# One-directional filter tiles with sums and differences of halves, and another order at front, gates and maxima

## The chip, the core and the metric

The kernel runs on one core of a Trainium2 chip. The metric is the device time of one execution in microseconds; the time before is a median of three runs. Five engines work side by side, each through its own instructions in order: TensorE (PE, with its weight loads on PEld), VectorE (DVE), ScalarE (ACT), GpSimd (POOL) and SyncE (SP, which issues nearly all of the transfers here). In this kernel PE's products go to PSUM, from where the other engines read them, and many matrix products are sums of products of high and low parts in the type fp32r.

## What is computed

Two layers over 1024 latent tokens of width 1024 with 256 context tokens. Layer 0 is attention (grouped-query heads and latent-attention heads side by side, a SiLU gate, one output projection), layer 1 is a Hyena mixer with long convolutions. The part that the change touches most makes the filters of these convolutions, which depend on no token:

```python
hid = sin(freq * (emb @ w1 + b1)); hid = sin(freq * (hid @ w2 + b2))
h = (hid @ w3 + b3).reshape(L, HY_ORDER, 2, HY_WIDTH)
h = h * exp(-t * abs(deltas))[:, None, None, :]
fwd, bwd = h[:, :, 0], h[:, :, 1]
kern = concatenate([fwd, zeros((1, HY_ORDER, HY_WIDTH)), bwd[:0:-1]], axis=0)   # 2048 taps
kern = kern / sum(abs(kern), axis=0, keepdims=True)
return rfft(kern, axis=0)
```

In attention, the scores of a group are exponentiated after a row maximum is taken off; the gate is `silu(h @ w_gate)`.

## The kernel before

**Filters (up to about 255 us).** A small MLP gives `hid` for the 1024 positions (`sin_arg` on DVE, Sin on ACT). `hidden(q)` puts it into tiles of 128 partitions, the forward positions in one half and the backward ones in the other, as high part `Hh` and low part `Hl`. The loop at L604 then runs over 38 steps: 8 blocks of 128 channels by 4 quarters of the taps, and 6 steps to drain. Step n does, on the engines in this order:

- `taps(n)` (L472): PE, four outputs of 128x256, each from four products: the bias `ind`·`b4` (L479) and the three of `mm3` (L100 to L102).
- `decay(n + 1)` (L530): ACT, four exponentials into `dec`, of which there are two buffers.
- `second_stage` and `spectra`: PE multiplies regrouped data by `FBk` (L572); DVE scales by the reciprocal norm into `kc` (L583), which is written to DRAM. This works on an earlier block.
- `decayed(n)` (L535): DVE, `kern` = taps times decay, 128x1024.
- `first_stage(n - 1)`: PE multiplies two halves of `kern` by `FKc` (L557), ACT copies to `aT` (L559).
- `norms(n)`: ACT takes absolute values of two halves (L544), POOL adds them up (L546, L550).
- a regrouping by DMA through SP, the reciprocal `rn` once per block (L647), and `split_coefs` once per block: high and low parts of `w3` and the bias (ACT L339 and L342, POOL L340, DVE L343). `coefs` loads them.

With each step go pieces of other work, pulled from generators. `mods` multiplies the adaLN weights (32 tiles of 512 KB through SP, `adaw`) on PE (L217); `PM` says how many of its pieces go where in the MLP, and one is pulled in each step. `stats` takes the tokens' norms in steps 0 to 11. `toks` prepares tokens from step 11 on: DVE scales a tile (L402), PE transposes half of it (L408), ACT modulates it in four pieces into `mraw` (L413), DVE casts it to the high part (L420), POOL makes the low part (L421). Steps 12 to 31 are called the token steps below.

**Gates (about 378 to 480 us).** Sixteen tiles, each of 24 products. `load(n)` fetches a weight tile, ACT casts it to `wh` (L803), POOL (n under 8) or DVE subtracts the low part `wl` (L804), all right before tile n - 1 is multiplied. The rotary work of POOL and DVE (L838, L839, L840) runs in the same stretch.

**Attention (about 480 to 1010 us).** 32 groups gi of five slices s. In the last slice (s = 4), `max_rows(gi + 1)` has PE transpose the next group's maxima `m` (L1023) between the two halves `scores(0)` and `scores(1)`; DVE has reduced them to `m` (L1008) just ahead. Once, near 745 us, the weights `uvr` of the values are scaled and cast on ACT and their low part `uvl` subtracted on POOL (L1508), before PE multiplies with it (L101).

The order of each engine is fixed when the program is built: a scheduler of streams takes the pieces by their costs and due times (`yield cost, delay`).

Of the kernel before, what the change touches and what calls it, by code (L numbers as in the profile page):

```python
# [2294 lines left out]
```

## Time and profile before

| | us |
|---|---|
| median of three runs (lowest, highest) | 1813.27 (1812.65, 1813.64) |
| profiled execution | 1815.76 |
| its span, first to last instruction | 1813.9 |
| PE busy in it | 1727.4 (95%) |
| DVE, ACT, POOL busy | 1075.8 (59%), 775.1 (43%), 819.9 (45%) |
| mean granted clock of PE | 0.984 |

The profiled execution lies 2.5 us above the median. The profile is read by stage: a view of stretches says which engine is full, a view of lines what one instruction takes, the view in order of time who waits for whom; the number in brackets is the idle time ahead of an instruction and its releaser. PE's matmuls overlap, so a duration of 0.28 us can stand at a distance of 0.12.

### The profile page before, as it was taken

The numbers are of one execution on the slowest core, as the hardware profiler recorded it, in microseconds if no ns is written. First come the engines' busy times: TensorE is split into PE (matmuls) and PEld (weight loads), VectorE is DVE, ScalarE is ACT, GpSimd is POOL, SyncE is SP. The second block draws the span as 40 slices with busy tenths as digits, with TensorE's granted clock in tenths as the row PEclk, the third lists the DMA queues.
The fourth block names the chain that finished last, engine by engine and source line by source line (L and its number), as shares of the span: only waits on it lengthen the run. The fifth ranks groups of instructions, "written<-read, shape, count | busy, mean of one in ns | idle before, by whom it ended". The sixth has DMA issues, their size and how long they took to land. (4 is left out here: it accounts for less than half of the span.)

```text
span 1813.9 us, 25833 instructions
## 1 busy us (share of the span) xinstructions
PE 1727.4 (95%) x9616; PEld 1349.0 (74%) x9616; DVE 1075.8 (59%) x1575; ACT 775.1 (43%) x1326; POOL 819.9 (45%) x583
## 2 busy tenths in 40 slices
PE   7889999998999999899999999999999999999898
PEld 2677788986766666566666788888888887888786
DVE  4557747636765666366656323555776667766843
ACT  3877721243545545544444333333333433333431
POOL 1457732434179777677777453233322223233200
PEclk8999999999999999999999999999999999999999
DMA  7766678322220010101001226556676675785533
GB/s 251 227 201 224 214 239 269 117 70 70 54 59 24 13 38 18 50 23 35 19 22 33 79 82 150 141 147 205 185 215 184 192 199 166 199 246 180 168 101 108
DMA packets 236493, 236.50 MB, mean 130 GB/s; under 512 B 29567, under 2 KB 194343, under 8 KB 235951
## 3 DMA queue, kind: packets, MB, share of 16 engines
q1 hardware_dynamic: 234192, 232.75, 42.4%
q10 hardware_dynamic: 2176, 2.10, 0.4%
q8 instruction: 76, 1.25, 0.3%
q14 instruction: 49, 0.40, 0.1%
HBM read 152.87 MB, written 61.94 MB: 118 GB/s over the span
## 5 line engine op out<-in xcount | busy, mean ns | idle before, releaser
L990 DVE TENSOR_REDUCE mx<-pq 128x1 f32<-128x512 f32 x256 | 170.8, 682 | 113.1 <-PE pq L989 111.2
L1294 ACT ACTIVATE PT<-pw 128x1024 f32<-128x1024 f32 x160 | 163.7, 1025 | 171.8 <-PE pw L1277 157.4
L100 PE MATMUL pw<-h1h,wh 128*128 128x512 f32 x512 | 208.9, 408 | 0.0
L102 PE MATMUL pw<-h1h,wl 128*128 128x512 f32 x512 | 201.6, 394 | 0.0
L101 PE MATMUL pw<-h1l,wh 128*128 128x512 f32 x512 | 200.3, 391 | 0.0
L1189 POOL TENSOR_TENSOR acc<-acc,PT 128x1024 f32<-128x1024 f32 x62 | 147.4, 2377 | 22.3 <-ACT PT L1294 20.7
L1712 POOL TENSOR_TENSOR wl<-wr,wh 128x1024 fp32r<-128x1024 f32 x32 | 76.9, 2405 | 139.8 <-ACT wh L1711 129.5
L102 PEld LDWEIGHTS pw<-h1h,wl 128*128 128x128 f32 x512 | 96.4, 188 | 21.4
L546 POOL TENSOR_TENSOR kacc<-kacc,kabs 128x512 f32<-128x512 f32 x56 | 72.4, 1293 | 86.9 <-ACT kabs L544 85.0
L101 PEld LDWEIGHTS pw<-h1l,wh 128*128 128x128 f32 x512 | 96.8, 189 | 17.8
L100 PEld LDWEIGHTS pw<-h1h,wh 128*128 128x128 f32 x512 | 96.8, 189 | 17.4
L1187 POOL TENSOR_TENSOR acc<-PT,PT 128x1024 f32<-128x1024 f32 x31 | 73.9, 2385 | 53.8 <-ACT PT L1294 50.5
L1847 POOL TENSOR_TENSOR K<-K,skp 128x512 f32<-128x512 f32 x32 | 42.5, 1330 | 122.4 <-DMA K<-Kd 119.9
L1860 DVE TENSOR_TENSOR cA<-pq,K 64x512 f32<-64x512 f32 x128 | 88.1, 688 | 1.8
L1856 DVE SCALAR_TENSOR_TENSOR cB<-pq,K 64x512 f32<-64x512 f32 x64 | 44.3, 693 | 73.5 <-PE pq L1853 37.1
L1827 ACT COPY caT<-pq 128x512 f32<-128x512 f32 x64 | 37.6, 588 | 117.3 <-PE pq L102 107.0
L572 PE MATMUL pq<-au,FBk 128*128 128x256 f32 x256 | 68.1, 390 | 12.1 <-DVE kc L583 10.6
L1875 ACT COPY cbT<-pq 128x512 f32<-128x512 f32 x64 | 37.5, 587 | 97.3 <-PE pq L1873 68.1
L1873 PEld LDWEIGHTS pq<-cA,GB 128*128 128x128 f32 x512 | 67.3, 193 | 15.0 <-issue 10.0
L1180 PE MATMUL pv<-PT,Va 128*64 128x256 f32 x640 | 77.9, 385 | 0.0
L1180 PE MATMUL pv<-PT,Vm 128*64 128x256 f32 x640 | 77.7, 385 | 0.0
L1873 PE MATMUL pq<-cA,GB 128*128 128x128 f32 x512 | 68.8, 278 | 7.6 <-DVE cA L1863 6.6
(450 smaller groups left out, 4730.6 us busy)
## 6 DMA issues: line engine op xcount, KB each, us to landing
au<-aT SPq DMA_DIRECT2D x128, 128.0 KB
space<-in_ada_w_dram SPq DMA_DIRECT2D x32, 512.0 KB
wr<-in_hy_w_in_dram SPq DMA_DIRECT2D x32, 512.0 KB
K<-Kd SPq DMA_DIRECT2D x64, 256.0 KB
ad<-caT SPq DMA_DIRECT2D x64, 256.0 KB
cau<-ad SPq DMA_DIRECT2D x32, 512.0 KB
bd<-cbT SPq DMA_DIRECT2D x32, 512.0 KB
spare<-bd SPq DMA_DIRECT2D x64, 256.0 KB
```

The costliest lines, as they stand in the source:

```text
L100: nc.tensor.matmul(ps, lh, rh, start=start, stop=False)
L101: nc.tensor.matmul(ps, lh, rl, start=False, stop=False)
L102: nc.tensor.matmul(ps, ll, rh, start=False, stop=stop)
L546: nc.gpsimd.tensor_tensor(accs[p], accs[p], ab, ALU.add)
L990: nc.vector.reduce_max(m[:, i, j:j + 1], ps, axis=AX.X)
L1180: nc.tensor.matmul(ps[64 * e:64 * e + 64, 0:256], vals[:, 2 * s + j], PT[:, j, 256 * e:256 * e + 256], start=s == 0 and j == 0, stop=s == ...
L1187: eng.tensor_tensor(accs[gi], prev, PT, ALU.add)
L1189: eng.tensor_tensor(accs[gi], accs[gi], PT, ALU.add)
L1294: nc.scalar.activation(PT, ps.rearrange("p (a q) -> p a q", q=512), AF.Exp, scale=SC_A if kind == 0 else SC_M)
L1712: nc.gpsimd.tensor_tensor(wl, f(r), f(wh), ALU.subtract)
L1860: nc.vector.tensor_tensor(A1[64 * e:64 * e + 64], pv[64 * e:64 * e + 64], K[:, 0], ALU.mult)
L1873: nc.tensor.matmul(ps[:, i * P:(i + 1) * P], GB[:, 4 * uc + i, :], A1[:, i, :], start=True, stop=True)
```

## The change

**Filters.** Each tile of taps now holds positions of one direction only (d is forward or backward), with all 128 partitions used for high and low part together: `HA` holds the high part in one half and the low part in the other, `HB` the high part and rows of ones. So an output takes two products (`HA`·`WA`, `HB`·`WB`) where it took four, 8 for 16 in a step. `halves` has POOL make the sum and the difference of the two directions, and `first_stage` multiplies these. The norm is one DVE reduction of absolute values per step, over four taps at a stride of 256 elements, and one POOL add. `dec` has one buffer, and its four exponentials are issued as two pairs, each ahead of an `aT` copy. `split_coefs` has six ACT casts for two, two POOL and two DVE subtractions, and comes a step later; `coefs` comes one block ahead.

**Front.** `PM` is smaller, `mods` is pulled twice in steps 0 to 2, and the parts of `hidden` are issued between the two `sin_arg`.

**Gates, maxima, values.** A raw gate tile is loaded one tile earlier, and POOL subtracts only for tiles 2, 4 and 6. In groups of odd gi, `max_rows` follows `scores(1)`. `uvl` is subtracted on DVE. Constants change with the layout.

```diff
-PM = 3, 3, 5, 3
+PM = 2, 1, 3, 3
...
     def split_coefs(p):
         w3r, b3r, dl = coef[p]
-        w3h = fp.tile([P, CB], F32R, tag="w3h", bufs=2, name=nm("w3h"))
-        w3l = fp.tile([P, CB], F32R, tag="w3l", bufs=2, name=nm("w3l"))
-        nc.scalar.copy(w3h, w3r)
-        nc.gpsimd.tensor_tensor(w3l, w3r, f(w3h), ALU.subtract)
-        b4 = b4s[p % 2]
-        nc.scalar.copy(b4[0:2], b3r)
-        nc.vector.tensor_tensor(b4[32:34], b3r, f(b4[0:2]), ALU.subtract)
-        coef[p] = w3h, w3l, b4, dl
+        wa = fp.tile([P, 2, CB], F32R, tag="WA", bufs=2, name=nm("WA"))
+        wb = WB[p % 2]
+        for i in range(2):
+            a = slice(64 * i, 64 * i + 64)
+            for h in (a, slice(64 - 64 * i, 128 - 64 * i)):
+                nc.scalar.copy(wa[h, i], w3r[a])
+            nc.gpsimd.tensor_tensor(wb[a, i], w3r[a], f(wa[a, i]), ALU.subtract)
+            b_ = 64 * (1 - i)
+            nc.scalar.copy(wb[b_:b_ + 1, i], b3r[b_:b_ + 1])
+            nc.vector.tensor_tensor(wb[b_ + 32:b_ + 33, i], b3r[b_:b_ + 1], f(wb[b_:b_ + 1, i]), ALU.subtract)
+        coef[p] = wa, wb, dl
...
         def taps(n):
             p, gq = steps[n]
-            w3h, w3l, b4, _ = coef[p]
+            wa, wb, _ = coef[p]
             pws[n] = pw()
             for i in range(4):
-                g = 4 * gq + i
+                d, g = i // 2, 2 * gq + i % 2
                 pv = pws[n][:, i * CB:(i + 1) * CB]
-                nc.tensor.matmul(pv, ind, b4, start=True, stop=False)
-                mm3(nc, pv, Hh[:, g], Hl[:, g], w3h, w3l, False, True)
+                nc.tensor.matmul(pv, HA[:, d, g], wa[:, d], start=True, stop=False)
+                nc.tensor.matmul(pv, HB[:, d, g], wb[:, d], start=False, stop=True)
...
         def hidden(q):
-            c = slice(8 * q, 8 * q + 8)
-            for h in hs:
-                nc.scalar.activation(Hr[h, c, h], args[q][h, :].rearrange("p (g m) -> p g m", m=64), AF.Sin)
-            nc.scalar.copy(Hh[:, c], Hr[:, c])
-            (nc.vector, nc.gpsimd)[q].tensor_tensor(Hl[:, c], Hr[:, c], f(Hh[:, c]), ALU.subtract)
-
+            c = slice(4 * q, 4 * q + 4)
+            a = args[q].rearrange("p (g m) -> p g m", m=P)
+            nc.scalar.activation(a, a, AF.Sin)
+            for d, h in enumerate(hs):
+                nc.scalar.copy(HA[h, d, c], a[h])
+                nc.gpsimd.tensor_copy(HB[h, d, c], HA[h, d, c])
+                nc.vector.tensor_tensor(HA[hs[1 - d], d, c], a[h], f(HA[h, d, c]), ALU.subtract)
+
+        split_coefs(0)
         args[1] = sin_arg(pss[1], b2)
-        nc.scalar.copy(ind, indr)
-        split_coefs(0)
+        hidden(1)
         args[0] = sin_arg(pss[0], b2)
-        hidden(1)
         hidden(0)
...
-        def decay(n):
+        def decay(n, d):
+
             if n < len(steps):
                 p, gq = steps[n]
-                decs[n] = fw.tile([P, 4, P], F32, tag="dec", bufs=2, name=nm("dec"))
-                for j in range(4):
-                    nc.scalar.activation(decs[n][:, j], coef[p][-1], AF.Exp, scale=tng[:, 4 * gq + j:4 * gq + j + 1])
+                if d == 0:
+                    decs[n] = fw.tile([P, 4, P], F32, tag="dec", bufs=1, name=nm("dec"))
+                for j in range(2 * d, 2 * d + 2):
+                    t = j // 2 * NT + 2 * gq + j % 2
+                    nc.scalar.activation(decs[n][:, j], coef[p][-1], AF.Exp, scale=tng[:, t:t + 1])
...
         def norms(n):
+
             p, gq = steps[n]
+            t = fw.tile([P, CB], F32, tag="kacc" if gq == 3 else "kabs", bufs=2 if gq == 3 else 1, name=nm("kabs"))
+            nc.vector.tensor_reduce(t, kns[n].rearrange("p (g c) -> p c g", g=4), AX.X, ALU.add, apply_absolute_value=True)
             if gq == 3:
-                accs[p] = fw.tile([P, 512], F32, tag="kacc", bufs=1, name=nm("kacc"))
-            for i in range(2):
-                ab = accs[p] if gq == 3 and i == 0 else fw.tile([P, 512], F32, tag="kabs", bufs=2, name=nm("kabs"))
-                nc.scalar.activation(ab, kns[n][:, 512 * i:512 * i + 512], AF.Abs)
-                if ab is not accs[p]:
-                    nc.gpsimd.tensor_tensor(accs[p], accs[p], ab, ALU.add)
+                accs[p] = t
+            else:
+                nc.gpsimd.tensor_tensor(accs[p], accs[p], t, ALU.add)
             if gq == 0:
-                acc = accs.pop(p)
-                sums[p] = fw.tile([P, CB], F32, tag="ksum", bufs=1, name=nm("ksum"))
-                nc.gpsimd.tensor_tensor(sums[p], acc[:, :CB], acc[:, CB:], ALU.add)
+                sums[p] = accs.pop(p)
+
+        def halves(n):
+
+            a, b = kns[n][:, :512], kns[n][:, 512:]
+            sds[n] = [fw.tile([P, 512], F32, tag=t, bufs=1, name=nm(t)) for t in ("sum", "dif")]
+            for t, op_ in zip(sds[n], (ALU.add, ALU.subtract)):
+                nc.gpsimd.tensor_tensor(t, a, b, op_)
...
             ps = pq()
-            nc.tensor.matmul(ps, FKc, kns[n][:, j * 512:(j + 1) * 512], start=True, stop=True)
-            g = 4 * gq + 2 * j
-            nc.scalar.copy(aTs[p][:, g:g + 2, :], ps.rearrange("p (g c) -> p g c", c=CB))
+            nc.tensor.matmul(ps, FKc[:, j], sds[n][j], start=True, stop=True)
+            nc.scalar.copy(aTs[p][:, j, 2 * gq:2 * gq + 2, :], ps.rearrange("p (g c) -> p g c", c=CB))
...
-            decay(n + 1)
             if n >= 6:
                 ps0 = second_stage(pb, ub, 0)
             if n < N:
                 decayed(n)
+            decay(n + 1, 0)
             if n >= 6:
                 spectra(pb, ub, 0, ps0)
             if 0 < n <= N:
                 first_stage(n - 1, 0)
+            decay(n + 1, 1)
+            if 0 < n <= N:
                 first_stage(n - 1, 1)
             if n < N:
+                halves(n)
                 norms(n)
...
-                if q == 1 and p + 1 < NT:
+                if q == 0 and p + 1 < NT:
+                    coefs(p + 1)
+                if q == 2 and p + 1 < NT:
                     split_coefs(p + 1)
-                if q == 2 and p + 2 < NT:
-                    coefs(p + 2)
             if n == 2:
                 nc.sync.dma_start(FBk, I["FBk"])
-            pull(mods)
+            pull(mods, 2 if n < 3 else 1)
...
-                    (nc.gpsimd if n < 8 else nc.vector).tensor_tensor(wl, r, f(wh), ALU.subtract)
+                    (nc.gpsimd if n in (2, 4, 6) else nc.vector).tensor_tensor(wl, r, f(wh), ALU.subtract)
...
-                load(n + 1)
+                split(n + 1)
+                load(n + 2)
...
-                if s == 4 and gi + 1 < 32:
+                if s == 4 and gi % 2 == 0:
                     max_rows(gi + 1)
-                    cost += 0.1
                 scores(1, todo)
+                if s == 4 and gi % 2 and gi + 1 < 32:
+                    max_rows(gi + 1)
...
-        nc.gpsimd.tensor_tensor(uvl, r, f(uvh), ALU.subtract)
+        nc.vector.tensor_tensor(uvl, r, f(uvh), ALU.subtract)
```

On PE at the front, before: the rest of the adaLN products ahead of the first taps (L217 `pada` from the loads `adaw`; L497 is the MLP; `pw` the taps' bank).

```order
L217 MATMUL pada_181<-adaw_178,sT 32x512 x2
L217 MATMUL pada_181<-adaw_182,sT 32x512 x2
L217 MATMUL pada_181<-adaw_186,sT 32x512 x2
L497 MATMUL pq_214<-h_40_212,w_131 64x512 x2
L217 MATMUL pada_181<-adaw_190,sT 32x512 x2
L217 MATMUL pada_181<-adaw_199,sT 32x512 x2
L217 MATMUL pada_181<-adaw_203,sT 32x512 x2
L217 MATMUL pada_181<-adaw_208,sT 32x512 x2
L217 MATMUL pada_181<-adaw_217,sT 32x512 x2
L479 MATMUL pw_269<-b_111,ind 128x256
L100 MATMUL pw_269<-w3h_247,Hh 128x256
```

And now:

```order
L499 MATMUL pq_189<-h_34_187,w_132 64x512 x2
L217 MATMUL pada_178<-adaw_173,sT 32x512 x2
L499 MATMUL pq_198<-h_37_196,w_132 64x512 x2
L217 MATMUL pada_178<-adaw_175,sT 32x512 x2
L217 MATMUL pada_178<-adaw_179,sT 32x512 x2
L217 MATMUL pada_178<-adaw_183,sT 32x512 x2
L483 MATMUL pw_256<-WA_215,HA 128x256
L484 MATMUL pw_256<-WB_110,HB 128x256
L483 MATMUL pw_256<-WA_215,HA 128x256
```

The first taps stand behind 6 loads of `adaw`, where they stood behind 11; five of them follow later.

On ACT in one token step, before (`mraw` the modulated token, `kabs` the absolute values):

```order
L530 ACTIVATE dec_1370<-dlt_874,tng 128x128 x4
L559 COPY aT_1305<-pq_1383 128x512 [waits PE_49]
L559 COPY aT_1305<-pq_1386 128x512 [waits PE_49]
L544 ACTIVATE kabs_1389<-kern_1378 128x512 [waits DVE_49,Pool_49]
L544 ACTIVATE kabs_1392<-kern_1378 128x512 [waits Pool_49]
L413 ACTIVATE mraw_1417<-pq_1412,shl_504,scl_505 128x128 [waits PE_49]
L413 ACTIVATE mraw_1417<-pq_1412,shl_504,scl_505 128x128 x3
```

And now, in a step that also splits the coefficients (`WA`, `WB`):

```order
L536 ACTIVATE dec_1254<-dlt_911,tng 128x128 [waits DVE_49,Activation_49]
L536 ACTIVATE dec_1254<-dlt_911,tng 128x128
L569 COPY aT_1195<-pq_1260 128x512 [waits PE_49]
L536 ACTIVATE dec_1254<-dlt_911,tng 128x128 x2
L569 COPY aT_1195<-pq_1265 128x512 [waits PE_49]
L345 CAST WA_1286<-w3r_1154 64x256 x2
L348 CAST WB_111<-b3r_1156 1x256 [waits DMAHW0_49]
L345 CAST WA_1286<-w3r_1154 64x256 x2
L348 CAST WB_111<-b3r_1156 1x256
L419 ACTIVATE mraw_1302<-pq_1297,shl_581,scl_582 128x128 [waits PE_49,Pool_49]
L419 ACTIVATE mraw_1302<-pq_1297,shl_581,scl_582 128x128 x3
```

The absolute values are gone, the decays stand in two pairs with a wait for DVE ahead of the first, and six casts lie between the second `aT` and the token.

On POOL where the low part `uvl` was made, before (L1189 adds up the exponentials of attention, L1250 scales an output):

```order
L1187 TENSOR_TENSOR acc_7009<-PT_6950,PT_6972 128x1024 [waits DVE_49,Activation_49]
L1189 TENSOR_TENSOR acc_7009<-acc_7009,PT_7004 128x1024 [waits Activation_49,Pool_49]
L1250 TENSOR_TENSOR gT<-gT,rb_6960 64x512 [waits DMAHW2_49,DVE_49,Pool_49]
L1508 TENSOR_TENSOR uvl<-uvr,uvh 128x512 [waits Activation_49,Pool_49]
L1524 MEMSET kc_6933 64x1280 [waits PE_49,Pool_49]
```

And on DVE now, with the reductions of maxima around it (L1010 and L1028, which were L990 and L1008):

```order
L1014 TENSOR_REDUCE mx_6746<-pq_6826 128x2 [waits PE_49]
L1010 TENSOR_REDUCE mx_6746<-pq_6830 128x1 [waits PE_49]
L1028 TENSOR_REDUCE m_1400_6834<-mx_6746 128x4 [waits DVE_49]
L1529 TENSOR_TENSOR uvl<-uvr,uvh 128x512 [waits Activation_49,Pool_49]
L1048 TENSOR_TENSOR QA_4442<-pq_6918,dneg 4x512 [waits PE_49]
```

The subtraction left a place behind two POOL instructions for one behind the reduction to `m`, with the same two inputs.

## Rows read from the trace of the kernel before

**Rows 1.** Stretch: length; busy us (instructions) of PE, PEld, DVE, ACT, POOL; clock; DMA
```profile
80.00:100.00 20.00, 15.09 (x74) 10.60 (x72) 9.07 (x10) 14.10 (x32) 7.81 (x8) 1.00 0.78 229
```

**Rows 2.** DVE in time: start, us, instruction [idle before <-releaser]; four products `kern`
```profile
30.98 1.22 DVE L535 TENSOR_TENSOR kern<-pw,dec 128x1024 f32<-128x1024 f32 x1 [1.29 <-ACT dec L530]
...
40.67 1.22 DVE L535 TENSOR_TENSOR kern<-pw,dec 128x1024 f32<-128x1024 f32 x1 [8.47 <-PE pw L102]
...
104.62 1.22 DVE L535 TENSOR_TENSOR kern<-pw,dec 128x1024 f32<-128x1024 f32 x1 [2.34 <-PE pw L102]
...
226.23 1.21 DVE L535 TENSOR_TENSOR kern<-pw,dec 128x1024 f32<-128x1024 f32 x1
```

**Rows 3.** In time, around the second step: decays, PE's adaLN product
```profile
33.30 1.26 ACT L530 ACTIVATE dec<-dlt,tng 128x128 f32<-128x128 f32 x4
...
35.92 1.14 PE L217 MATMUL pada<-adaw,sT 128*32 128x512 f32 x4 [3.56 <-DMA adaw<-in_ada_w_dram]
```

**Rows 4.** In time, one token step: taps, token copies
```profile
140.02 0.28 PE L479 MATMUL pw<-b,ind 128*128 128x256 f32 x1
...
140.49 0.28 PE L479 MATMUL pw<-b,ind 128*128 128x256 f32 x1
...
146.31 1.51 ACT L413 ACTIVATE mraw<-pq,shl,scl 128x128 f32<-128x128 f32 x4 [0.47 <-PE pq L408]
```

**Rows 5.** Groups by line, 40 to 255 us: busy, mean ns | idle, releasers
```profile
L583 DVE TENSOR_TENSOR kc<-pq,rn 128x512 f32<-128x512 f32 x64 | 43.6, 686 | 50.4 <-PE pq L572 28.7 <-DMA Kd<-kc 18.9 <-PE pq L557 2.6
...
L535 DVE TENSOR_TENSOR kern<-pw,dec 128x1024 f32<-128x1024 f32 x31 | 37.8, 1218 | 22.7 <-PE pw L102 19.5 <-ACT kabs L544 1.8 <-ACT kacc L544 0.6
...
L559 ACT COPY aT<-pq 128x512 f32<-128x512 f32 x64 | 36.8, 584 | 44.3 <-PE pq L557 42.5 <-DMA au<-aT 1.8
...
L420 DVE CAST h<-mraw 128x256 fp32r<-128x256 f32 x32 | 18.5, 603 | 10.3 <-ACT mraw L413 10.2
L647 DVE RECIPROCAL rn<-pq 128x256 f32<-128x256 f32 x8 | 14.1, 1758 | 1.6 <-PE pq L635 0.9
...
L402 DVE TENSOR_SCALAR xt<-xt,rr 128x1024 f32<-128x1024 f32 x10 | 10.3, 1035 | 0.0
...
L339 ACT CAST w3h<-w3r 128x256 fp32r<-128x256 f32 x7 | 2.8, 399 | 0.0
```

**Rows 6.** One line's reduction: min/median/max ns, first and last start
```profile
L907 DVE TENSOR_REDUCE ssq<-hsq x4: 1219/1220/1222, 383.2 to 392.2; 128x16 f32<-128x1024 f32 x4
```

**Rows 7.** PE in time: a wait in a token step
```profile
196.60 0.66 PE L408 MATMUL pq<-ident,xt 128*128 128x128 f32 x4 [2.05 <-DVE kc L583]
...
197.01 0.41 PE L479 MATMUL pw<-b,ind 128*128 128x256 f32 x1
...
200.42 0.90 PE L572 MATMUL pq<-au,FBk 128*128 128x256 f32 x3
```

**Rows 8.** In time, gates: POOL and DVE side by side, PE's wait
```profile
406.90 2.39 POOL L804 TENSOR_TENSOR wl<-wr,wh 128x1024 fp32r<-128x1024 f32 x1
406.97 3.40 DVE L840 TENSOR_TENSOR pD<-rt,rt 128x1024 f32<-128x1024 f32 x1 [2.72 <-POOL rt L838]
...
418.90 0.69 PE L102 MATMUL pw<-h,wl 128*128 128x512 f32 x1 [3.69 <-POOL wl L804]
...
433.56 1.23 DVE L840 TENSOR_TENSOR pD<-rt,rt 128x1024 f32<-128x1024 f32 x1 [2.73 <-POOL rt L838]
```

**Rows 9.** In time, the weights `uvl`: POOL, DVE and PE
```profile
747.21 2.35 POOL L1189 TENSOR_TENSOR acc<-acc,PT 128x1024 f32<-128x1024 f32 x1 [2.56 <-ACT PT L1294]
...
748.15 0.17 DVE L1008 TENSOR_REDUCE m<-mx 128x4 f32<-128x12 f32 x1
...
752.30 0.79 PE L101 MATMUL pq<-uvl,ckh 128*128 128x512 f32 x1 [4.17 <-POOL uvl L1508]
```

**Rows 10.** PE's waits in attention: total us, times, longest
```profile
PE pq L1023 <- DVE m L1008: 6.7, 13, 0.8
```

**Rows 11.** PE in time: transpose of maxima, odd gi
```profile
781.42 0.27 PE L1023 MATMUL pq<-ident,m 128*4 128x128 f32 x1 [0.38 <-DVE m L1008]
```

More of the change, by code (lines that the diff above doesn't have):

```diff
@@ L316, in backbone @@
     CB = 256
-    b4s = [fp.tile([P, CB], F32R, tag=f"b4{i}", name=f"b4{i}") for i in range(2)]
-    for b4 in b4s:
-        nc.vector.memset(f(b4), 0.0)
+    WB = [fp.tile([P, 2, CB], F32R, tag=f"WB{i}", name=f"WB{i}") for i in range(2)]
+    for w in WB:
+        nc.vector.memset(f(w), 0.0)
+    nc.vector.memset(f(HB[64:128, 0]), 1.0)
+    nc.vector.memset(f(HB[0:64, 1]), 1.0)
     coef = {}
@@ L579, in spectra @@
             if tail and u0 % 8 > 3:
-                kc = fw.tile([P, 4, P], F32, tag="dec", bufs=2, name=nm("kc")).rearrange("p (h u) c -> p h u c", h=2)
+                kc = fw.tile([P, 4, P], F32, tag=("sum", "dif")[u0 // 2 % 2], bufs=1, name=nm("kc")).rearrange("p (h u) c -> p h u c", h=2)
             else:
@@ L585, in spectra @@
             (nc.scalar if tail else nc.sync).dma_start(Kd[:, p, :, u0 * P:(u0 + 2) * P].rearrange("h p f -> p h f"), kc.rearrange("p h u c -> p h (u c)"))
-        coefs(1)
-        decay(0)
+        decay(0, 0)
+        decay(0, 1)
         N = len(steps)
@@ L793, in gates @@
         with pool("wg") as wp:
-            wt = {}
+            wt, raw = {}, {}
             def load(n):
@@ L803, in load @@
                     nc.scalar.copy(wh, r)
-                    (nc.gpsimd if n < 8 else nc.vector).tensor_tensor(wl, r, f(wh), ALU.subtract)
+                    (nc.gpsimd if n in (2, 4, 6) else nc.vector).tensor_tensor(wl, r, f(wh), ALU.subtract)
                     wt[n] = wh, wl
+            load(1)
             wt[0] = box["g0"][1:]
@@ L2159, in constants @@
             FA[j + 8 * t2, :, j * 16 + np.arange(16)] = F_[t2]
-    FK = np.zeros((P, P))
-    F_ = stage_a(32)
-    for j in range(4):
-        for t2 in range(32):
+    FK = np.zeros((P, 2, P))
+    F_ = stage_a(16)
+    h = np.arange(8)
+    for j in range(8):
+        for t2 in range(16):
             for p in range(2):
-                FK[j + 4 * t2, (np.arange(16) % 4 * 8 + p * 4 + j) * 4 + np.arange(16) // 4] = F_[t2, :, p]
+                for e in range(2):
+                    FK[j + 8 * t2, e, (p * 8 + j) * 8 + h % 2 * 4 + h // 2] = F_[t2, 2 * h + e, p]
     t1 = np.arange(64)
@@ L2206, in constants @@
             IA[j * 16 + u][:, j + 8 * t2] = a / 2048
-    g, m = np.meshgrid(np.arange(16), np.arange(P), indexing="ij")
-    n = g + 16 * m
-    tok = np.where(n < 1024, n, (2048 - n) % 1024)
+    d, g, m = np.meshgrid(np.arange(2), np.arange(8), np.arange(P), indexing="ij")
+    n = g + 8 * m
+    tok = np.where(d == 0, n, (1024 - n) % 1024)
     t = np.linspace(0.0, 1.0, 1024).astype(np.float32)
@@ L2216, in constants @@
     emb = np.concatenate([t[:, None].astype(np.float64), np.cos(ang), -np.sin(ang)], axis=1)
-    tneg = np.where(n == 1024, -1e30, -t[tok].astype(np.float64)).T
-    e = emb[tok]
-    emb2 = np.stack([e[:, :64].reshape(1024, 33), e[:, 64:].reshape(1024, 33)]).transpose(2, 0, 1)
+    tneg = np.where((d == 1) & (n == 0), -1e30, -t[tok].astype(np.float64)).reshape(16, P).T
+    emb2 = emb[tok].reshape(2, 1024, 33).transpose(2, 0, 1)
     lo, hi = np.log(1e-2) / 1.5, np.log(1e-2) / 0.3
     absd = np.abs(np.linspace(lo, hi, 1024))
-    ind = np.zeros((P, P))
-    for b in (0, 32):
-        ind[b, :64] = 1.0
-        ind[b + 1, 64:] = 1.0
     pos = (np.arange(8)[:, None] + 8 * np.arange(P)[None, :])
@@ L2275, in arrays_of @@
     a["w3"] = np.ascontiguousarray(np.asarray(inputs["hy_ffn_w3"])[0].reshape(64, 2, 2, NT, P).transpose(3, 2, 0, 1, 4).reshape(NT, P, 2 * P))
-    a["b3"] = np.ascontiguousarray(np.asarray(inputs["hy_ffn_b3"])[0].reshape(2, 2, NT, P).transpose(2, 1, 0, 3).reshape(NT, 2, 2 * P))
+    a["b3"] = np.ascontiguousarray(np.asarray(inputs["hy_ffn_b3"])[0].reshape(2, 2, NT, P).transpose(2, 1, 0, 3)[:, ::-1].reshape(NT, 2, 2 * P))
     a.update(constants())
```

35 lines of the change are left out of this document (17 added, 18 removed).

## The prediction

> **What bounds the kernel now.** No share of busy time answers this, since the change touches three stages with different limits; I read, in this order, the stretches, the `kern` products as the clock of the filter loop, the groups by line, and the order of time around each wait of PE.
>
> In the filters' middle steps PE is not full: from 80 to 100 us it works 15.09 of 20 us at granted clock 1.00 while the DMA share is 0.78 [rows 1], so these steps wait in part for the adaLN transfers. The `kern` products stand at 30.98, 40.67, 104.62 and 226.23 us for steps 0, 1, 12 and 31 [rows 2]: 9.7 us for step 0, (104.62 - 40.67) / 11 = 5.81 us for each of steps 1 to 11, (226.23 - 104.62) / 19 = 6.40 us for each token step. Ahead of step 1 DVE stood idle for 8.47 us, until PE's taps came [rows 2], and these stood behind an adaLN product that waited 3.56 us for its load [rows 3]. In the token steps a chain over DVE, PE and ACT runs close to PE's own work, and `kern` at 226.23 shows no wait. Behind the filters only three places count: PE's 3.69 us for a gate weight [rows 8], its 4.17 us for `uvl` [rows 9], and 6.7 us in 13 waits for maxima [rows 10].
>
> **Front.** The first taps pass five loads, and the second taps now need 11 loads where they needed 15. So the wait on the load at 35.92 us [rows 3] no longer stands ahead of them. What is late next is ACT: with one buffer, the decay of step 1 follows `kern` of step 0. I take step 0's `kern` 0.8 us later than now, since the second half of the Sin argument on DVE stands behind the first half's subtractions, which wait for ACT (this is a judgement; bounds 0 and 2.5): 30.98 + 0.8 + 1.22 + 1.26 for four decays [rows 2, 3] = 34.3, and a handover. Step 1 at 34.4 instead of 40.67: **-6** (-4 to -7).
>
> **Middle steps, n = 2 to 10.** Two taps matmuls four apart lie 0.47 us apart, 0.118 us each [rows 4]; eight fewer save 0.94 us of PE per step. If the idle quarter stays, nine steps give -8.5. If the transfers alone set the pace, 0; if shorter steps also lose half of the 1.4 us of idle time (a quarter of 5.81), -14. I take **-8**: PE's work is three quarters of the step, so this is nearest to the first. POOL's sums and differences replace as many additions of the same shape; ACT's absolute values go, where ACT did not bind.
>
> **Token steps, 12 to 31.** PE is relieved by the same 0.94 us, but the chain changes. ACT's first decay pair waits for this step's `kern` (it shares its one buffer), and behind that wait ACT's whole queue stands: first `aT`, second pair, second `aT`, then the token's four pieces, which DVE must cast before it comes to the next `kern`. The chain: `kern` 1.22, pair 0.63 [rows 3], `aT` 0.58, pair 0.63, `aT` 0.58 [rows 5], token 1.51 [rows 4], last cast 0.60, on every second step the scaling `xt` 1.04, so 0.52 [rows 5]: 6.27. Every fourth step six casts for the coefficients lie ahead of the token; at 0.31 each (the nearest row is 0.40 for a cast twice as tall [rows 5], and pieces issued in a row overlap) 1.86, so 0.47 a step. Sum 6.74, against 6.40: 0.34 x 19 = **+7**. The lower bound is DVE alone: `kern` 1.22, two `kc` 1.37, the new reduction 1.22 (128x1024 into sixteens [rows 6]), two casts 1.21, half of `xt` 0.52, a quarter of `rn` 0.44 [rows 5] = 5.98, so -8. The upper bound: a handover of 0.1 us at four places, +0.4 x 19 = 8 more, +15. That the transposes' and `kc`'s part of the loop is faster than ACT's is assumed. The drain after step 31 I set at nothing (2 us either way): its regrouping is the same.
>
> **Gates.** If the wait at 418.90 goes, 3.69 us go, and with the slow clock behind it (the matmul there takes 0.69 us) up to 5 [rows 8]. But the rotary work now shares DVE with the subtractions, and shares it badly: the same product took 1.23 us alone and 3.40 us when POOL had begun a subtraction 0.07 us before it [rows 8]; POOL ended at 409.29 and DVE 1.08 us later, so DVE stood for nearly all of POOL's time. I take **-2** (-5 to +1).
>
> **Values `uvl`.** DVE is free at 748.15 + 0.17 = 748.32, and a product of this shape takes it 0.69 [rows 5, 9], so PE could start at 749.05, 3.25 us earlier, and lose less clock (-5.4 with that). But both inputs lie in SBUF, as in the gates' row, and POOL's addition runs until 747.21 + 2.35 = 749.56 [rows 9]. If DVE stands until then, PE starts at 750.3: 2.0 earlier. I take **-2.5** (-2 to -5.4), nearer the second because of the row with 3.40.
>
> The Trainium skill, "SBUF — State Buffer", section "Who interferes with whom", says that a DVE instruction with two SBUF inputs contends with a GpSimd instruction that reads SBUF and that the loser blocks fully. The 3.40 us agree with it; by the rule this term is -2.0, without it -3.25 or more.
>
> **Maxima.** Of 13 waits, all in groups of odd gi, seven, in the latent heads, last 0.38 like the one shown, and the other six 0.67 on average, (6.7 - 2.7) / 6 [rows 10, 11]. Behind the transpose come now two or three matmuls fewer, ahead of it as many more, 0.23 us each: 0.46 of each long wait and all of the short ones, 2.8 + 2.7 = **-5.4** (-4 to -6.7). DVE's product behind it comes later, but a burst of 16 matmuls lies ahead of the scores that need it.
>
> **The sum.** -6 - 8 + 7 + 0 - 2 - 2.5 - 5.4 = -17 against the profiled execution's 1815.8: 1798.9. The median of the runs shown is 2.5 lower: **1796**. The unknown terms move independently; their ends, squared and added, give some 19 down and 12 up.
>
> **Rivals.**
>
> *Fast token steps.* The chain over ACT doesn't bind, since the pieces of decay and `aT` slip into waits; DVE's own 5.98 us are the pace. For it: in the middle of the loop ACT was far from full. Against it: one buffer makes ACT wait for `kern` in every step. Token term -8 for +7: 1781 (1776 to 1787).
>
> *The reduction over a stride.* It reads four values 1 KB apart for each result; the row of 1.22 us reads in another order. If it took twice that, 2.44, DVE's work per token step would be 7.20: 0.46 more than the chain, 19 x 0.46 = 9, and about 5 more in the middle steps, which have no room left on DVE. 1796 + 14 = 1810. No row here shows such a read. The Trainium skill, "Advanced Engine Details and Errata", section "SBUF Cachelines", says that accesses which each fall on a different 16-byte line pay a penalty and gives no price; by it this rival would be the forecast.
>
> *Slower: the clock.* In a token step PE waited 2.05 us for `kc`, and the 16 taps behind it took 200.42 - 197.01 = 3.41 us, 0.213 each, the lower of the clock's two levels, 1.2 GHz [rows 7]. With 0.94 us less work in a longer step (6.74), PE idles some two microseconds in each. If that takes its clock, a step at half clock costs between 0.76 more (its 8 taps) and 2 x (6.40 - 0.94) - 6.74 = 4.2 more (if PE worked through the whole step before); middle 2.5. From seven such steps on the whole gain is gone; ten give +25, 1821. Against it: at three quarters busy the clock stayed at 1.00 [rows 1].
>
> *The waits move.* Gates, `uvl` and maxima give nothing, since PE meets another wait just behind: 1796 + 10 = 1806.
>
> **Chances.** Forecast 0.54 (1787 to 1808), fast token steps 0.17, the stride 0.10, the clock 0.13, moved waits 0.06. Range 1776 to 1812: it leaves out the clock's case and the tails of the other two. A measurement here tells 0.2% (3.6 us) from no change: below 1809.6 lie the forecast, the fast case, the moved waits and a fifth of the stride's: faster 0.79; same 0.08; slower 0.13.
>
> **What would show it.** Right: `kern` of step 1 near 34.4, of step 12 near 90, then 6.5 to 7 us apart with the idle time of DVE put down to the token's pieces on ACT; the taps at 8 per step; the reduction near 1.22; PE's wait for `uvl` near 2; waits for `m` together under 1.5 us. Wrong: `kern` under 6.2 apart in the token steps (fast), a reduction of 2 us or more (stride), granted clock under 0.9 from 110 to 230 us (clock), or new waits at 410 to 430 and 750 us of the old size.

## The result, and the profile after

The changed kernel takes 1792.76 us (median of four, 1791.5 to 1793.92), the kernel before, on the same chip, 1812.96 (1809.1 to 1813.64): a ratio of 0.9908, 95% interval 0.9889 to 0.9928, so 20 us or 0.9% less. The prediction said 1796, range 1776 to 1812. Its total is near. Of its terms three are near what was measured (token steps, gates, maxima), the front has the right size for a wrong reason, the middle steps gave less than half of theirs, the values' reason did not hold, and the drain, set at nothing, differs by scatter.

The page's first lines show the profiled execution: a span 24 us shorter than the 1813.9 of before.

```profile
span 1789.9 us, 25447 instructions
...
PE 1698.6 (95%) x9360; PEld 1313.9 (73%) x9360; DVE 1136.4 (63%) x1625; ACT 751.7 (42%) x1293; POOL 837.1 (47%) x612
```

PE's busy time fell by 28.8 us; DVE's rose by 60.6 us, which the new reduction and the subtractions brought. The products `kern` of steps 0, 1, 12 and 31 answer to [rows 2]:

```profile
32.19 1.23 DVE L541 TENSOR_TENSOR kern<-pw,dec 128x1024 f32<-128x1024 f32 x1 [1.53 <-ACT dec L536]
...
35.30 1.22 DVE L541 TENSOR_TENSOR kern<-pw,dec 128x1024 f32<-128x1024 f32 x1
...
95.65 1.16 DVE L541 TENSOR_TENSOR kern<-pw,dec 128x1024 f32<-128x1024 f32 x1
...
223.80 1.21 DVE L541 TENSOR_TENSOR kern<-pw,dec 128x1024 f32<-128x1024 f32 x1
```

Step 0 is 1.2 us later, step 1 is 5.4 us earlier, step 12 is 9.0 earlier and step 31 only 2.4. So the front and the middle steps gained, and the token steps gave most of it back, as forecast. The view of stretches shows the steps 1 to 6 and the token steps of before and then of after (columns as in [rows 1]):

```profile
40.67:62.65 21.98, 21.98 (x118) 15.20 (x116) 11.30 (x15) 20.92 (x49) 11.96 (x11) 1.00 0.69 235
104.62:226.23 121.61, 117.29 (x621) 89.90 (x621) 85.74 (x108) 92.79 (x233) 80.46 (x77) 0.98 0.67 212
```

```profile
35.30:59.24 23.94, 23.01 (x92) 10.64 (x91) 19.53 (x15) 18.65 (x46) 17.66 (x17) 0.94 0.81 268
95.65:223.80 128.15, 109.78 (x467) 74.43 (x466) 114.45 (x132) 80.79 (x217) 94.96 (x96) 0.93 0.70 207
```

The token steps take 128.15 us for 121.61: 6.74 us each for 6.40. PE's work in them fell by 7.5 us and DVE's rose by 29, to 89%.

The groups by line, 40 to 255 us, answer to [rows 5, 6]:

```profile
L548 DVE TENSOR_REDUCE kabs<-kern 128x256 f32<-128x1024 f32 x30 | 59.7, 1989 | 0.3
...
L426 DVE CAST h<-mraw 128x256 fp32r<-128x256 f32 x32 | 13.3, 429 | 5.6 <-ACT mraw L419 5.5
...
L408 DVE TENSOR_SCALAR xt<-xt,rr 128x1024 f32<-128x1024 f32 x10 | 7.4, 742 | 0.0
```

The reduction takes 1.99 us, where the contiguous one of before, another sum over as many elements, took 1.22 [rows 6]. The casts and the scaling became shorter than before (0.43 for 0.60, 0.74 for 1.04).

Behind the filters, first and last starts of four groups tell the stages apart: the gates' SiLU (sixteen), the cast of `uvr`, the ten copies of `Vm`, the exponentials. After:

```profile
L840 ACT ACTIVATE gT<-pw x16: 582/599/604, 381.6 to 480.3; 128x512 f32<-128x512 f32 x16
...
L1527 ACT CAST uvh<-uvr x1: 608/608/608, 734.1 to 734.1; 128x512 fp32r<-128x512 f32 x1
...
L1535 ACT COPY Vm<-pq x10: 586/589/590, 738.3 to 744.4; 128x512 f32<-128x512 f32 x10
...
L1315 ACT ACTIVATE PT<-pw x160: 1012/1026/1031, 484.6 to 987.6; 128x1024 f32<-128x1024 f32 x160
```

The gates last 98.7 us (101.8 before: 387.3 to 489.1), attention to the cast 249.5 (253.6: 493.4 to 747.0), the values up to the last copy 10.3 (14.4: to 761.4), the rest up to the last exponential 243.2 (246.9: to 1008.3). From there to the end it is 802.3 us, for 805.6; this part is the same code, and it took 800 to 806 us in the twelve traces of this study, whatever was changed ahead of it, so these 3.3 us say nothing of the change.

The span's 24.0 us are so made up: steps 0 and 1 -5.4, steps 1 to 12 -3.6, token steps +6.5, from step 31 to the first SiLU -3.3, gates -3.1, attention -4.1, values -4.1, attention again -3.7, and the rest -3.3 by scatter.

### The profile page after: what moved, and what is told of

It reads as the page before. It is cut to its first block, busy times and chain, and to the rows that moved or that the text cites. A ratio compares the mean times of both kernels' runs of the same rounds, so it can differ in the third digit from the quotient of the medians.

```text
span 1789.9 us, 25447 instructions
## 1 busy us (share of the span) xinstructions
PE 1698.6 (95%) x9360; PEld 1313.9 (73%) x9360; DVE 1136.4 (63%) x1625; ACT 751.7 (42%) x1293; POOL 837.1 (47%) x612
## 3 DMA queue, kind: packets, MB, share of 16 engines
q8 instruction: 74, 1.21, 0.3%
## 5 line engine op out<-in xcount | busy, mean ns | idle before, releaser
L1010 DVE TENSOR_REDUCE mx<-pq 128x1 f32<-128x512 f32 x256 | 170.9, 682 | 100.4 <-PE pq L1009 98.6
L1894 PEld LDWEIGHTS pq<-cA,GB 128*128 128x128 f32 x512 | 67.3, 193 | 15.3 <-issue 10.3
L1911 DVE TENSOR_TENSOR cil<-spare,cih 128x512 fp32r<-128x512 f32 x64 | 53.8, 879 | 34.8 <-ACT cih L1910 34.6
```

What stands on the lines that cost most here:

```text
L1010: nc.vector.reduce_max(m[:, i, j:j + 1], ps, axis=AX.X)
L1894: nc.tensor.matmul(ps[:, i * P:(i + 1) * P], GB[:, 4 * uc + i, :], A1[:, i, :], start=True, stop=True)
L1911: nc.vector.tensor_tensor(il, r, f(ih), ALU.subtract)
```

## Experiments

The theory as the prediction had it: in the token steps ACT's chain sets the pace (decay pairs, `aT`, the coefficients' casts, the token's pieces). The rival, which the trace of after suggests: the slow reduction fills DVE, and DVE sets it. In the view of a step that splits coefficients (order of time, DVE and ACT) both can be seen:

```profile
163.63 1.22 DVE L541 TENSOR_TENSOR kern<-pw,dec 128x1024 f32<-128x1024 f32 x1
...
164.94 0.69 ACT L536 ACTIVATE dec<-dlt,tng 128x128 f32<-128x128 f32 x2 [2.80 <-DVE kern L541]
...
167.07 0.84 ACT L345 CAST WA<-w3r 64x256 fp32r<-64x256 f32 x2
...
169.40 1.48 ACT L419 ACTIVATE mraw<-pq,shl,scl 128x128 f32<-128x128 f32 x4
...
170.91 0.62 DVE L426 CAST h<-mraw 128x256 fp32r<-128x256 f32 x1 [0.39 <-ACT mraw L419]
...
172.12 1.21 DVE L541 TENSOR_TENSOR kern<-pw,dec 128x1024 f32<-128x1024 f32 x1
```

ACT waits for `kern`, then runs with hardly a gap from 164.94 to 170.88 (`aT`, the second decay pair and `aT` follow the first pair; the six casts lie from 167.07 to 169.49), and DVE waits 0.39 us for the token's last pieces; 8.49 us lie between the two `kern`. But DVE is nearly full in the other steps.

**The reduction made contiguous.**

```diff
-            nc.vector.tensor_reduce(t, kns[n].rearrange("p (g c) -> p c g", g=4), AX.X, ALU.add, apply_absolute_value=True)
+            nc.vector.tensor_reduce(t, kns[n].rearrange("p (c g) -> p c g", g=4), AX.X, ALU.add, apply_absolute_value=True)
```

> The changed kernel with the norms' reduction over four neighbouring elements instead of four taps 1 KB apart: same count of elements, contiguous (it changes which values are summed, so the norms are other numbers). Theory A (the stride costs 0.77 us, and DVE is what fills a token step): the reduction falls from 1.99 to about 1.22 us, token steps from 6.74 to 6.0 to 6.2 us, 10 to 14 us in all. Rival B (the chain over ACT's decay pairs sets the step, as the prediction had it): the reduction falls as much, but token steps stay at 6.5 to 6.75 and the time falls under 4 us.

1787.62 us (before, same chip, 1808.18), ratio 0.9893 (0.9873 to 0.9914): not to be told from the changed kernel's 0.9908. It adds up neighbouring channels instead of the taps of one channel, so its norms are other numbers: it is a probe of time and no kernel to use. The token steps, and the reduction in them:

```profile
94.38:219.19 124.81, 107.91 (x467) 73.90 (x466) 101.45 (x133) 80.42 (x217) 94.93 (x96) 0.95 0.72 212
```

```profile
L548 DVE TENSOR_REDUCE kabs<-kern 128x256 f32<-128x1024 f32 x17 | 20.5, 1205 | 0.0
```

0.78 us less of DVE in each step shortened the step by 0.18 on average, to 6.57 (three other traces with the filters of the changed kernel have 6.68 to 6.74). Eleven of the nineteen steps stayed as they were to a tenth, and the four long ones of 8.3 to 8.5 us to a hundredth. So the stride's price is real, and for the most part it lies beside the chain.

**The taps stored interleaved**, so that the price moves from the reduction, which then reads neighbours, to the product; POOL then reads at the stride:

```diff
             v = "p (g o c) -> p g o c"
-            nc.vector.tensor_tensor(kns[n].rearrange(v, g=4, o=2), pws.pop(n).rearrange(v, g=4, o=2),
+            nc.vector.tensor_tensor(kns[n].rearrange("p (o c g) -> p g o c", g=4, o=2), pws.pop(n).rearrange(v, g=4, o=2),
...
```

> The changed kernel with the filter taps stored interleaved: the reduction reads contiguously, the product of taps and decay writes at a stride of 16 bytes, POOL's halves read at that stride. If the stride of reads costs on DVE alone: reduction 1.22, product 1.21 and POOL 1.28 as they were, token steps 6.0 to 6.2 us. If writing or POOL's reading pays instead: the product or the halves take 1.5 times as long or more, and token steps are no shorter than 6.7.

One run, 1807.25 us. Its groups by line, and its token steps:

```profile
L541 DVE TENSOR_TENSOR kern<-pw,dec 128x1024 f32<-128x1024 f32 x16 | 31.8, 1987 | 0.0
...
L548 DVE TENSOR_REDUCE kabs<-kern 128x256 f32<-128x1024 f32 x16 | 19.3, 1206 | 0.0
L562 POOL TENSOR_TENSOR dif<-kern 128x512 f32<-128x512 f32 x16 | 18.3, 1142 | 0.0
```

```profile
99.17:235.51 136.34, 108.97 (x464) 75.34 (x463) 111.64 (x133) 79.63 (x216) 89.14 (x96) 0.92 0.64 191
```

The reduction became 1.21 us, and the product, which now writes every fourth element, 1.99: the same 0.78 us, paid at another place. POOL reads at the same stride in 1.14 us, less than the 1.28 of the changed kernel. The sum of DVE's work is nearly unchanged, and yet a step takes 7.18 us instead of 6.74, since `kern` is a link of the chain and the reduction is not. Together with the run above this speaks for the chain; the total rests on one run, the step on its trace.

**The casts behind the token's pieces.** The bias is cast one step earlier, `WA` behind `mraw`:

```diff
                 if q == 2 and p + 1 < NT:
-                    split_coefs(p + 1)
+                    bias_low(p + 1)
...
+            if n < N and p + 1 < NT:
+                if q == 1:
+                    bias_high(p + 1)
+                if q == 2:
+                    split_coefs(p + 1)
```

> The changed kernel with the casts for the next block's coefficients moved behind the token's pieces on ACT (the bias's casts one step earlier, DVE's bias subtractions where the casts were, with nothing left to wait for). Theory A (in the step that splits, ACT's six casts stand ahead of the token's pieces and set the step): the four long steps of 8.3 to 8.5 us (14, 18, 22, 26) fall to 6.0 to 6.6, token steps from 6.74 to about 6.3 on average, 8 to 9 us in all, more if the three splits in the middle steps count too. Rival B (DVE alone fills the steps): the long steps fall by under 1 us and their neighbours grow, under 3 us in all.

1785.08 us beside 1804.78 (ratio 0.9893, 0.9857 to 0.9929). The long steps fell from 8.3 to 8.5 us to 7.8, 6.9, 6.9 and 6.9, and the token steps to 6.26 on average. The gain of 9.1 us in the token steps is what theory A of the expectation gave (8 to 9); the long steps fell less than it said (to 6.0 to 6.6). To see it beside the changed kernel, both ran again on one chip, with a third kernel that has the contiguous reduction too:

> The changed kernel as it is, beside the two below on one chip. The ratio to the kernel before should come again at 0.989 to 0.993, with token steps of 6.74 us.

> The kernel with the casts moved behind the token's pieces, again, against the changed kernel on the same chip. Theory: its token steps of 6.26 us against 6.74 and its end of the filters 9 us earlier are a gain of the kernel: 7 to 10 us less than the changed kernel's time. Rival: the earlier end is given back in the stages behind; then the two agree within 3 us.

> The casts moved and the reduction contiguous together (the norms are sums of neighbouring channels, so other numbers). If DVE fills the steps once the casts are out of the way: the reduction at 1.21 instead of 1.99 us takes 0.5 to 0.77 us from each token step, 6.26 to 5.5 to 5.8. If ACT's chain (1.21 + 0.69 + 0.56 + 0.69 + 0.56 + 1.51 and the last cast, 5.6 to 5.7, and 0.37 for the scaling on average) is right behind it: 5.9 to 6.1.

| kernel | us (lowest, highest) | ratio to before, 95% |
|---|---|---|
| changed | 1791.61 (1790.42, 1795.77) | 0.9910 (0.9886, 0.9934) |
| casts moved | 1785.71 (1780.39, 1787.83) | 0.9871 (0.9848, 0.9894) |
| casts moved, contiguous | 1780.07 (1774.31, 1784.36) | 0.9841 (0.9811, 0.9872) |

The changed kernel's ratio came again; in microseconds its gain is 15.4 here (before: 1807.03). With the casts moved, all runs lie below all of the changed kernel's; the medians differ by 5.9 us, less than the 7 to 10 expected and more than the rival's 3. In the two traces the last `kern` of the filters stands 9.8 us earlier, and gates and attention take the same time to a tenth. The kernel with moved casts beats both the changed kernel and the one before; the third, with its other norms, is a probe again. The same step as above, with the casts moved (order of time):

```profile
157.51 1.22 DVE L554 TENSOR_TENSOR kern<-pw,dec 128x1024 f32<-128x1024 f32 x1
...
160.96 1.51 ACT L430 ACTIVATE mraw<-pq,shl,scl 128x128 f32<-128x128 f32 x4
...
162.34 1.70 ACT L345 CAST WA<-w3r 64x256 fp32r<-64x256 f32 x4
...
164.42 1.21 DVE L554 TENSOR_TENSOR kern<-pw,dec 128x1024 f32<-128x1024 f32 x1
```

The four `WA` casts start when the token's pieces are done, and the next `kern` is 6.91 us away. The token steps of the two kernels with moved casts, the second with the contiguous reduction:

```profile
95.06:214.54 119.48, 103.17 (x467) 69.57 (x466) 113.95 (x133) 81.19 (x217) 95.13 (x96) 0.99 0.77 232
```

```profile
93.45:212.06 118.61, 102.92 (x467) 69.51 (x466) 101.85 (x133) 81.19 (x217) 95.39 (x96) 0.99 0.78 234
```

DVE's work fell by 12 us, from 95% to 86%, and the stretch by 0.9: 6.29 and 6.24 us a step, where DVE as the bound would have given 5.5 to 5.8. One step of the second, from 14 to 15, took 9.6 us; without it the steps behind average 6.15 against 6.29. I read from this that ACT's chain and DVE end nearly together once the casts are away; taking from DVE alone no longer paid much. What the third kernel's smaller median is made of, beyond these steps, was not followed up.

**Taking from DVE in earnest.** The token's scaling on ACT, the bias subtractions on POOL:

```diff
-            nc.vector.tensor_scalar(xt, xt, rr[:, t:t + 1], 0.0, ALU.mult, ALU.add)
+            nc.scalar.activation(xt, xt, AF.Copy, scale=rr[:, t:t + 1])
```

> As the kernel with moved casts, and also the scaling of the token tile on ACT instead of DVE (0.74 us on every second step) and the bias subtractions on POOL (0.7 us twice per block); the casts all come one step earlier. Theory A with DVE as the next bound: token steps 5.9 to 6.2 us, some 3 to 6 us less than with the casts moved alone. Rival: ACT's chain is next, its added 1.05 us lies in the way of the next decay pair, and the time is the same as with the casts moved alone or worse.

1787.04 us (ratio 0.9896, 0.9865 to 0.9927), no better than the casts moved alone on that chip (1785.08). DVE's casts took longer again:

```profile
L440 DVE CAST h<-mraw 128x256 fp32r<-128x256 f32 x32 | 18.9, 612 | 3.0 <-ACT mraw L433 3.0
```

0.61 us for 0.42: part of what DVE no longer did came back as longer casts. The trace shows beside what:

```profile
159.84 0.42 DVE L440 CAST h<-mraw 128x256 fp32r<-128x256 f32 x2
...
170.68 1.26 POOL L577 TENSOR_TENSOR dif<-kern 128x512 f32<-128x512 f32 x1
170.72 2.11 DVE L440 CAST h<-mraw 128x256 fp32r<-128x256 f32 x2
```

Two casts begun with POOL idle took 0.42 us; two begun 0.04 us behind POOL's difference took 2.11 us, until 172.83, and POOL's next addition ended at 172.68. Two other steps, of 9.5 and 9.7 us, contain a wait of DVE for a transfer, 2.3 and 2.5 us. So the outcome is the rival's, no gain, but its reason (ACT's scaling in the way of the next decay pair) is not what these rows show.

**The norms on PE and ACT**, so that DVE is left with an addition:

```diff
-            nc.vector.tensor_reduce(t, kns[n]..., AX.X, ALU.add, apply_absolute_value=True)
+            nc.scalar.activation(kns[n], kns[n], AF.Abs)
...
+                nc.tensor.matmul(ps[:, :CB], ones, kns[n][:, g * CB:(g + 1) * CB], start=g == 0, stop=g == 3)
```

> The changed kernel with the norms taken off DVE: ACT makes the absolute values in place (about 1.05 us, behind the token's pieces), PE sums them with ones in four more products per step (about 0.86 us), DVE adds 128x256 (about 0.4 us). If DVE fills the token step (theory A): steps of 5.8 to 6.2 us, 10 to 15 us less in all, about 1780. If the chain over ACT or PE binds first: steps of 6.5 or more and no gain.

1814.57 us, ratio 1.004 (1.002 to 1.0061): slower than before. The waits in 107 to 224 us:

```profile
ACT mraw L419 <- PE pq L414: 14.9, 12, 2.0
DVE kacc L562 <- PE pq L552: 14.0, 12, 1.6
```

The token steps took 7.32 us. The sums took PE 1.89 us a step, twice what was expected, and stood ahead of the transposes, so that ACT waited for these with the token's pieces (14.9 us in all, 3.6 in the changed kernel) and DVE for the sums. PE's slack in a token step was not free: it lies at one place of the chain.

**The front as before.**

```diff
-PM = 2, 1, 3, 3
+PM = 3, 3, 5, 3
...
-            pull(mods, 2 if n < 3 else 1)
+            pull(mods)
```

> The changed kernel with the front's adaLN pieces as before (3, 3, 5, 3 and one per step). Theory: the product of step 1 comes again at 39.5 to 41 us instead of 35.3, and the middle steps give a part of it back since they carry three pieces less; the time rises by 2 to 5 us. Rival: what was gained at the front is paid in the middle steps in full (the transfers set the pace): step 12 stands at 95.7 us as now, the time is the same.

1792.07 us (ratio 0.9925, 0.9902 to 0.9948). The second `kern`:

```profile
35.55 1.22 DVE L541 TENSOR_TENSOR kern<-pw,dec 128x1024 f32<-128x1024 f32 x1
```

0.25 us later than with the change, where the prediction's cause would have put it at 39.5 to 41. Step 12 stands at 95.1 as well. So the order of the adaLN pieces gave nothing that shows.

**Gates, maxima and `uvl` as before**, on the new filters and front:

```diff
-                    (nc.gpsimd if n in (2, 4, 6) else nc.vector).tensor_tensor(wl, r, f(wh), ALU.subtract)
+                    (nc.gpsimd if n < 8 else nc.vector).tensor_tensor(wl, r, f(wh), ALU.subtract)
...
-                if s == 4 and gi % 2 == 0:
+                if s == 4 and gi + 1 < 32:
                     max_rows(gi + 1)
+                    cost += 0.1
                 scores(1, todo)
-                if s == 4 and gi % 2 and gi + 1 < 32:
-                    max_rows(gi + 1)
...
-        nc.vector.tensor_tensor(uvl, r, f(uvh), ALU.subtract)
+        nc.gpsimd.tensor_tensor(uvl, r, f(uvh), ALU.subtract)
```

> The changed kernel with gates, maxima and uvl as before; only filters and front are new. Theory: the time rises by what the landmarks of the two traces give to these three, about 3 (gates) + 5 (maxima) + 4 (uvl) = 12 us, to some 1805; the stretch up to the first gate stays 5.7 us shorter than before. Rival: part of the gain behind the filters belongs to the earlier start of the stage and not to the three edits; then under 8 us come back.

1804.29 us beside 1808.18 (ratio 0.9987, 0.997 to 1.0004): nearly the whole gain is gone, and what is left is not told from nothing. PE's waits, at the gates and behind them:

```profile
PE pw L102 <- POOL wl L818: 4.8, 2, 3.7
...
PE pq L1037 <- DVE m L1022: 6.7, 13, 0.8
PE pq L101 <- POOL uvl L1522: 2.9, 1, 2.9
```

At the gates and for the maxima these are the waits of before to the tenth (4.8 and 6.7); for `uvl` PE waited 2.9 us here and 4.2 before. The stages, by the same four groups as above:

```profile
L834 ACT ACTIVATE gT<-pw x16: 583/599/605, 380.0 to 482.0; 128x512 f32<-128x512 f32 x16
...
L1520 ACT CAST uvh<-uvr x1: 608/608/608, 738.5 to 738.5; 128x512 fp32r<-128x512 f32 x1
...
L1528 ACT COPY Vm<-pq x10: 586/589/589, 745.2 to 752.3; 128x512 f32<-128x512 f32 x10
...
L1308 ACT ACTIVATE PT<-pw x160: 1011/1025/1032, 486.3 to 999.3; 128x1024 f32<-128x1024 f32 x160
```

Gates 102.0 us, attention to the cast 252.2, values 13.8, the rest 247.0: 3.3, 2.7, 3.5 and 3.8 longer than with the change, 13.3 together. These three small edits, not the filters, carry the gain: filters and front together gave some 2 to 4 us, with an interval that reaches zero.

## Why the prediction came out right, term by term

**Front, -6.** Measured -5.4, and the cause was wrong. The step that failed is "the second taps now need 11 loads where they needed 15": with 15 again, `kern` of step 1 still came at 35.55. In that run the taps are eight products instead of sixteen and the first ones began at 25.23 us (27.13 before); the run of six loads issued from 18.5 us (18.1 before) ended at 27.8 (31.9 before), and PE's wait for the load ended at 32.70 where it had ended at 35.92. That this comes from the halved taps and the order of `hidden` is what is left; it was not tried apart. What was late next was not ACT's decay, as the prediction had it, but the new reduction on DVE, which the sum for step 1 does not contain:

```profile
33.45 1.93 DVE L548 TENSOR_REDUCE kabs<-kern 128x256 f32<-128x1024 f32 x1
```

It stands between the `kern` of step 0 and that of step 1, with no idle time around it (the decays had ended at 34.73, the taps' products before 31), and step 1 came 3.11 us behind step 0. With the contiguous reduction it came 2.57 us behind, which is `kern` (1.22), four decays (1.28) and a handover: there the decay is the later one.

**Middle steps, -8.** Measured -3.6 up to step 12, so the sign "step 12 near 90" failed (95.65). The step that failed is "eight fewer save 0.94 us of PE per step. If the idle quarter stays, nine steps give -8.5": no stretch of the trace shows this saving. The idle quarter was read from 80 to 100 us, and before, PE had no idle time at all in 40.67 to 62.65 (21.98 of 21.98). Steps 1 to 6 took 23.94 us for 21.98, 2.0 more, where three to four less were expected. The excess lies in step 1 (5.53 us for 4.72) and step 2 (6.45 for 3.64), which splits coefficients; there DVE waited for ACT's casts ahead of the next `kern`:

```profile
45.51 0.87 DVE L349 TENSOR_TENSOR WB<-b3r,WB 1x256 fp32r<-1x256 f32 x1 [1.37 <-ACT WB L348]
```

With the casts moved, step 2 took 5.08 and 5.38 us. In steps 1 to 6 transfers rose from 235 to 268 GB/s and the granted clock fell from 1.00 to 0.94. Neither the contiguous reduction (24.2 us) nor the old front (24.4) shortened the stretch, moving the casts took 0.5 to 0.8 off, and both edits of the reduction and the casts together 2.0 (21.95); what binds there besides stays open. Steps 6 to 12 took 36.41 us (59.24 to 95.65) for 41.97 (62.65 to 104.62). That is 0.93 a step, the forecast's size, but by luck: steps 6 to 10 took 31.09 for 31.65, and step 11 alone 5.32 for 10.32. Before, DVE and then PE had waited in it for a transfer, and in the trace of after no such wait stands there. Whether the change removed it is not shown: with the casts moved, a step of 9.2 to 10.8 us stands one step earlier. The wait of before:

```profile
99.55 0.69 DVE L583 TENSOR_TENSOR kc<-pq,rn 128x512 f32<-128x512 f32 x1 [4.02 <-DMA Kd<-kc]
```

**Token steps, +7.** Measured +6.5, and a step of 6.74 us by forecast and by measurement. The chain is confirmed as the main bound: the casts' share was set at 0.47 us a step and moving them took 0.45 on one chip (6.74 to 6.29); lengthening a link by 0.78 (`kern`) cost 0.43 a step although the reduction became as much shorter in the same run, and shortening the reduction alone by 0.78 gave 0.18. If DVE alone set the step, the interleaved taps would have cost nothing and the contiguous reduction would have given 0.78. The fast token steps of the first rival did not come. A second buffer for the decay, which would try the chain at its root, was not tried. Errors inside the sum cancelled: the scaling and the casts were shorter than set (0.74 and 0.43 for 1.04 and 0.60, so 0.32 a step); 0.18 of this went to the longer reduction, and the rest I put down to handovers, which no run measures apart. The lower bound, DVE's work at 5.98, came out near (114.45 / 19 = 6.02), again since errors cancelled: the reduction took 0.77 more than set.

**The stride.** This rival's mechanism is there, at 1.99 us for 1.21 contiguous: 0.78 more, where the rival supposed 1.22 more; the sign "the reduction near 1.22" failed. The Trainium skill, "Advanced Engine Details and Errata", section "SBUF Cachelines", has the penalty, and the trace agrees in kind; on POOL's reads (1.14 us at a stride of 16 bytes) no run shows it. It did not decide the time, because the reduction stands beside the chain.

**The clock.** It fell to 0.93 in the token steps (0.98 before; 0.99 with the casts moved), so the rival's sign, under 0.9, did not come. As a mean of the two levels, 0.93 would be some 14% of the stretch at the lower one (an estimate from this row), about 18 us or under three steps; the rival needed seven.

**Drain, nothing.** From step 31 to the first SiLU it is 3.3 us shorter, 157.8 for 161.1. The second trace of the same changed kernel has 160.2, and the twelve traces have 157.3 to 161.3, so these 3.3 us say nothing of the change either.

**Gates, -2.** Measured -3.1 to -3.3. The large wait fell to 2.09 us (PE's waits at the gates together from 7.5 to 5.8), and the slow pair of the forecast is there once, where it was there three times before:

```profile
410.32 2.34 POOL L822 TENSOR_TENSOR wl<-wr,wh 128x1024 fp32r<-128x1024 f32 x1
410.38 3.36 DVE L860 TENSOR_TENSOR pD<-rt,rt 128x1024 f32<-128x1024 f32 x1 [2.74 <-POOL rt L858]
...
412.71 0.50 PE L102 MATMUL pw<-h,wl 128*128 128x512 f32 x1 [2.09 <-POOL wl L822]
```

DVE's product took 3.36 us again beside POOL's subtraction. It happens less often, since POOL subtracts three tiles; alone the product took 1.22.

**Values, -2.5.** Measured -3.5 to -4.1. The step that failed is "If DVE stands until then": POOL's addition did not lie across DVE's subtraction this time.

```profile
734.36 2.38 POOL L1209 TENSOR_TENSOR acc<-acc,PT 128x1024 f32<-128x1024 f32 x1 [1.23 <-ACT PT L1315]
...
736.70 0.69 DVE L1529 TENSOR_TENSOR uvl<-uvr,uvh 128x512 fp32r<-128x512 f32 x1
736.82 1.72 POOL L1270 TENSOR_TENSOR gT<-gT,rb 64x512 f32<-64x512 f32 x1
...
737.44 0.50 PE L101 MATMUL pq<-uvl,ckh 128*128 128x512 f32 x1 [0.85 <-DVE uvl L1529]
```

POOL's addition ended at 736.74, DVE began at 736.70 and took its plain 0.69 us; it was POOL's next instruction, begun 0.12 us behind DVE, that took 1.72 (1.26 before). PE waited 0.85 us for `uvl` and its matmuls behind stayed 0.23 us apart. So the bound without contention (-3.25 to -5.4) was the right one; the contention is there, and it fell on the other engine, for which PE was not waiting. The Trainium skill, "SBUF — State Buffer", section "Who interferes with whom", has it that the order of issue decides who blocks; the trace agrees, with 3.36 us on DVE at the gates and 1.72 on POOL here.

**Maxima, -5.4.** PE's waits for `m` are now

```profile
PE pq L1043 <- DVE m L1028: 1.3, 6, 0.3
```

5.4 us less than 6.7. The stages gained 2.7 + 3.8 = 6.5 by the run with the three edits undone.

Together, measured less forecast in the trace of after: +0.6 (front), +4.4 (middle), -0.5 (token), -3.3 (drain), -1.1 (gates), -1.6 (values), -2.4 (attention), so -3.9 beside the -17 forecast, and -3.3 of scatter at the end. Without the two stretches that scatter, the drain and the end, the measured terms sum to -17.5. That the total came so near is luck in part: the middle steps gave 4.4 us less than forecast, and gates, values and attention 5.1 more.

## What to carry to other kernels

A step that several engines share is costed by its chain: list which instruction waits for which, engine by engine in issue order, and add up; the same 0.78 us cost 0.18 us a step beside the chain and 0.43 or more in it. What has no hurry on an engine of the chain (here the next block's casts) belongs behind the urgent pieces, which was worth 6 us. Waits of PE on a short subtraction or reduction are cheap to remove by place and engine, and three such edits brought 13 us here.
